# A two-layer trunk with product-key experts on one core: operands of the expert selection in PSUM, sixteen conditioning items in an earlier stage, and the last norm dealt to more engines

## The chip, the cores and the metric

The kernel runs on one core of a Trainium2 chip. The metric is the device time of one execution in microseconds. The engines are named as in the profile: PE (TensorE), DVE (VectorE), ACT (ScalarE), POOL (GpSimd), SP (SyncE, which here issues most of the DMAs).

## What is computed

The model takes 256 prompt tokens and 32 sample tokens of width 1024 through two layers, all in float32. Cut to what matters here:

```python
for l in range(2):
    mod = silu(c) @ ada_w[l] + ada_b[l]              # 1024 x 6144 per layer, for two vectors c
    sh1, sc1, g1, sh2, sc2, g2 = split(mod, 6)
    h = modulate(rmsnorm(x, norm_mix[l]), sh1, sc1)
    x = x + g1 * (rglru_block(h) if l == 0 else conformer_conv_block(h))
    h = modulate(rmsnorm(x, norm_ffn[l]), sh2, sc2)
    x = x + g2 * peer(h)
y = rmsnorm(x, norm_final)

def peer(h):                                         # 8 heads, 128 + 128 keys, 16384 experts
    q = h @ w_q
    s1v, s1i = top_k(q[first half] @ k1.T, 16);  s2v, s2i = top_k(q[second half] @ k2.T, 16)
    sv, si = top_k(s1v[:, None] + s2v[None, :], 16)  # 16 of 256 pairs
    e = s1i[si // 16] * 128 + s2i[si % 16]
    return sum over the 16 of  softmax(sv) * gelu(u[e] . h) * v[e]
```

The kernel does not gather experts for the prompt. It computes z = h U^T for all 16384 experts, multiplies by a gate that is zero except at the selected ones, and multiplies by V. Only the sample tokens are gathered.

## The kernel before

**Items.** The program is one list of items, each of which brings a block of weights (512 KB for most) and multiplies it. `run_stream` walks the list as a pipeline: `load` issues the DMA on SP into one of three `raw` buffers; `prep`, two items ahead, transposes on DVE (z items, L955); `split`, one item ahead, makes a rounded high part on ACT (`hi`, L332) and the rest on POOL or DVE (`lo`, L333); then PE multiplies (hi by hi and lo, lo by hi, L342; for v items L1089); then `post` follows. The order in which Python emits instructions is each engine's order. Dependencies become semaphore waits.

**Threads.** Small side work (a list of operations with an engine, a cost and the number of items to wait before the next, the "hop") is emitted between items by `run_threads`, within a budget of time per engine and item.

**Conditioning.** `ada_unit(l, u, ring)` makes eight items for one of the six 1024-column parts of `ada_w[l]`: each has a load of 512 KB (L399) and two small products (L406); after the eighth a thread of copies (ACT), transposes (PE) and additions (DVE) finishes the part. These items have rings of their own (`rb` nine slots, `rc` six) and no place in the list: `with_ada(items, units, {k: n}, {k: (n, ahead)})` hangs n of them behind item k ("riding"), or n in front of it ("lead"). A riding item's load is issued when a slot is free, that is, when PE has read the slot's former content.

**The stages.** First 16 ada items. Then layer 0's LRU stage `d`: 8 items for the recurrent half of `w_in`, 8 for its gate half, 8 for `w_out`; ada items ride on items 2 to 9, and 8 lead item 16, the first of `w_out`. Then `peer_items(0, ...)`: 128 z items, which multiply the rows of U; behind each of z items 1 to 8 come two items of `w_q`, after which a thread takes the top 16 of one head and half; from z item 9 on, two ada items ride on each while there are some left. Here these are 24 (parts 5 of layer 0, 0 and 1 of layer 1): seven lead z item 0, seventeen ride.

**Selection.** When all top-16 results are there, the thread of `select_ops` runs while z items go on: candidates (POOL), top 16 of them (DVE), `conv` (subtracts the maximum, L776), the exponential (ACT), `start1` (L783 to L792), steps that turn positions into keys (L798, L801), `soft` (L811), `ints` (L818 to L822), `start2` (from L826), the same steps for the second key, two transposes (PE), `parts` (which splits the gate into mantissa and exponent, L856 to L862, and copies a constant, `iota4`) and `fin`, which starts 64 groups of gate work (L913). Its arrays are 128 x 288 and lie in `scr`, in SBUF; two of them, `far["pos"]` and `far["tmp"]`, lie in PSUM. Every operation is made in two halves.

**Experts down and the end.** 128 v items follow; four PSUM accumulators `acc[tt][half]` hold 128 tokens by 512 columns. The last two v items hold back the products for tt = 1, and after those for tt = 0 do them half by half. In layer 1, after the last item, each of the four quarters gets its gate, residual (`sums`: L1198, L1201) and squares (L1204, ACT); `inv_rms` makes 1/rms (L1213, L1215); `weighted` multiplies by the norm's weight (L1853), `y_out` by 1/rms (L1856, L1858), and three stores go out on SP (L1878, L1882). Layer 1 is built in the same way; where its own ada items stand is not changed.

## Time and profile before

| | |
|---|---|
| three runs | 2065.05, 2055.79, 2060.77 us; median 2060.77 |
| profiled execution | 2065.36 us; its span 2063.6 us, granted clock 0.989 |
| PE busy | 1989.8 us, 96% of the span (13603 instructions) |
| PE weight loads | 1718.6 us, 83% |
| DVE | 1534.8 us, 74% (3324) |
| ACT | 1113.3 us, 54% (1973) |
| POOL | 993.7 us, 48% (644) |
| read from memory | 434.19 MB, 213 GB/s over the span |

The profiled execution is one on the chip, a little longer than the median of the three. A view of windows gives, for stretches of time, how long each engine was busy, the granted clock of PE and the DMA engines' mean busy share. A timeline lists instructions with their start, their duration, how many were joined into a row and, in brackets, how long the engine stood before and what released it. A view of lines groups the instructions of the whole run by their line in the program.

### The profile page before, as it was taken

Reading aid. Unit: us, or ns where it says so; the run is one execution under the profiler, and the core shown is the slowest. Engines: PE = TensorE matmul, PEld = TensorE weight load, DVE = VectorE, ACT = ScalarE, POOL = GpSimd, SP = SyncE. Lnnn points to the kernel's source line nnn. Section 1 sums busy time; section 2 is a strip of 40 time slices with the busy share of each in tenths; the row PEclk is TensorE's granted clock in tenths of the full one; section 3 lists DMA queues with packets and bytes.
Section 4 is the critical chain, followed back from the end, with each engine's and each line's share of the span. In section 5 each row is a group of like instructions: output and inputs, shape, how many; then the busy total and the mean of one; then the engine's idle time right before and its main releaser. Section 6 shows DMA issues by size and latency. Waiting matters only on the chain.

```text
span 2063.6 us, 38013 instructions
## 1 busy us (share of the span) xinstructions
PE 1989.8 (96%) x13603; PEld 1718.6 (83%) x13603; DVE 1534.8 (74%) x3324; ACT 1113.3 (54%) x1973; POOL 993.7 (48%) x644
## 2 busy tenths in 40 slices
PE   6989999999999999999999899999999999999998
PEld 4777978999999887777877679999999988777776
DVE  5785559999998876455658855799999978754455
ACT  3655434478886444344554544444888854444444
POOL 4346667777775232121245266877777743312100
PEclk9999999999999999999999999999999999999999
DMA  9856595555556988887686455665555578878863
GB/s 341 274 180 217 142 247 163 168 171 158 156 155 220 314 297 284 291 278 235 236 271 163 148 161 147 179 174 164 169 158 155 157 259 315 296 276 293 277 202 124
DMA packets 311483, 444.44 MB, mean 215 GB/s; under 512 B 29326, under 2 KB 248126, under 8 KB 310782
## 3 DMA queue, kind: packets, MB, share of 16 engines
q1 hardware_dynamic: 292142, 374.73, 57.6%
q0 software_dynamic: 18976, 67.22, 9.4%
q8 instruction: 107, 1.75, 0.4%
q14 instruction: 82, 0.67, 0.1%
q10 hardware_dynamic: 176, 0.07, 0.0%
HBM read 434.19 MB, written 4.87 MB: 213 GB/s over the span
## 4 chain that ended last, share of the span: by engine, by line
PE 65%; DVE 11%; issue 9%; DMA 8%; POOL 5%; ACT 2%; SPq 1%; DVEq 0%; ACTq 0%; POOLq 0%
PE b L342 34%; PE acc L1089 21%; DVE ut L955 3%; PE acc L913 3%; POOL scr L996 3%; POOL lo L333 2%; DMA raw<-in_peer_u_dram 2%; DMA raw<-in_peer_v_dram 2%; PE b L1033 1%; DMA big<-in_ada_w_dram 1%; DVE lo L333 1%; ACT hi L332 1%; PE acc L406 1%; DMA scr<-in_peer_u_dram,eidx 1%; DVE acc L798 1%
## 5 line engine op out<-in xcount | busy, mean ns | idle before, releaser
L342 PE MATMUL b<-rnd,hi 128*128 128x256 f32 (+1 forms) x5376 | 737.9, 290 | 19.7 <-ACT hi L332 10.8
L333 POOL TENSOR_TENSOR lo<-ut,hi 128x1024 fp32r<-128x1024 f32 x253 | 608.1, 2406 | 231.7 <-PE b L342 122.2
L342 PEld LDWEIGHTS b<-rnd,hi 128*128 128x128 f32 x5376 | 681.1, 190 | 42.2 <-ACT hi L332 15.8
L332 ACT CAST hi<-raw 128x1024 fp32r<-128x1024 f32 x336 | 353.1, 1052 | 396.7 <-DMA raw<-in_peer_v_dram 234.0
L1089 PE MATMUL acc<-hi,rnd 128*128 128x512 f32 x2048 | 557.6, 393 | 2.9 <-ACT hi L332 2.7
L333 DVE TENSOR_TENSOR lo<-raw,hi 128x1024 fp32r<-128x1024 f32 x282 | 348.1, 1236 | 265.0 <-PE acc L1089 124.7
L1089 PEld LDWEIGHTS acc<-hi,rnd 128*128 128x128 f32 x2048 | 380.2, 188 | 111.9 <-issue 23.4
L955 DVE STREAM_TRANSPOSE ut<-raw 128x1024 f32<-128x1024 f32 x256 | 317.0, 1239 | 129.4 <-DMA raw<-in_peer_u_dram 97.2
L342 PE MATMUL b<-rnd,lo 128*128 128x256 f32 (+1 forms) x2688 | 386.4, 285 | 9.6 <-POOL lo L333 5.2
L342 PEld LDWEIGHTS b<-rnd,lo 128*128 128x128 f32 x2688 | 351.2, 189 | 14.3 <-POOL lo L333 8.8
L332 ACT CAST hi<-ut 128x1024 fp32r<-128x1024 f32 x256 | 269.5, 1053 | 172.2 <-DVE ut L955 148.8
L1089 PE MATMUL acc<-lo,rnd 128*128 128x512 f32 x1024 | 317.7, 391 | 1.7 <-DVE lo L333 1.3
L1089 PEld LDWEIGHTS acc<-lo,rnd 128*128 128x128 f32 x1024 | 191.2, 188 | 46.6 <-DVE lo L333 6.8
L1023 POOL DMA_INDIRECT big<-in_peer_v_dram,eidx x64 | 65.6, 1025 | 266.0 <-PE b L1033 252.8
L333 POOL TENSOR_TENSOR lo<-raw,hi 128x1024 fp32r<-128x1024 f32 x54 | 129.9, 2407 | 113.0 <-PE b L342 60.1
L996 POOL DMA_INDIRECT scr<-in_peer_u_dram,eidx x64 | 84.2, 1316 | 187.3 <-DVE scr L1000 186.6
L907 ACT ACTIVATE scr<-scr 128x128 bf16<-128x128 bf16 x512 | 169.3, 407 | 0.0
L976 ACT ACTIVATE big<-b 128x512 f32<-128x512 f32 (+32 forms) x123 | 59.8, 486 | 73.4 <-PE b L342 73.2
L1000 DVE SCALAR_TENSOR_TENSOR scr<-scr 128x1024 f32<-128x1024 f32 x64 | 78.1, 1221 | 25.9 <-DMA scr<-in_peer_u_dram,eidx 25.7
L1064 DVE TENSOR_TENSOR rnd<-big,rnd 128x512 fp32r<-128x512 f32 x128 | 89.9, 702 | 4.1 <-ACT rnd L1063 4.1
L913 PE MATMUL acc<-scr 128*128 128x128 bf16 x1024 | 81.9, 223 | 0.0
L1063 ACT CAST rnd<-big 128x512 fp32r<-128x512 f32 x128 | 78.8, 615 | 4.0 <-PE b L342 4.0
(316 smaller groups left out, 1593.6 us busy)
## 6 DMA issues: line engine op xcount, KB each, us to landing
raw<-in_peer_u_dram SPq DMA_DIRECT2D x1024, 128.0 KB
raw<-in_peer_v_dram SPq DMA_DIRECT2D x256, 512.0 KB
big<-in_ada_w_dram SPq DMA_DIRECT2D x96, 512.0 KB
raw<-in_peer_w_q_dram SPq DMA_DIRECT2D x128, 128.0 KB
raw<-in_cf_w_pw_dram SPq DMA_DIRECT2D x24, 512.0 KB
raw<-in_lru_w_in_dram SPq DMA_DIRECT2D x16, 512.0 KB
raw<-in_lru_w_out_dram SPq DMA_DIRECT2D x8, 512.0 KB
xsave<-big SPq DMA_DIRECT2D x2, 1152.0 KB
```

The lines of the kernel that those rows point to most:

```text
L332: S.copy(hi, src)
L333: (G if pool_lo else V).tensor_tensor(lo, src, hi.bitcast(F32), op=ALU.subtract)
L342: TE.matmul(ps, w[wi][:, c * P:(c + 1) * P], a[ai][:, c, :n], start=(start and wi == c == ai == 0), stop=(stop and wi == 1 and c == C - 1))
L907: S.activation(bt[:, j], b4[:, :, j], AF.Copy, scale=sexp[:, t0 + j:t0 + j + 1])
L913: TE.matmul(s["ps"][:, j * P:(j + 1) * P], a[:, :, j], bt[:, j], start=a is hi, stop=a is lo)
L955: V.transpose(s["ut"].rearrange("p (b e n) -> p e b n", b=8, e=4), s["raw"].rearrange("p (e b n) -> p e b n", e=4, b=8))
L996: G.indirect_dma_start(out=gt, out_offset=None, in_=Uf, in_offset=bass.IndirectOffsetOnAxis(ap=eidx[:, s:s + 1], axis=0))
L1000: V.scalar_tensor_tensor(gt, gt, 1.0, hs_v, op0=ALU.mult, op1=ALU.mult, accum_out=zs[:, s:s + 1])
L1023: G.indirect_dma_start(out=gt[j], out_offset=None, in_=Vf, in_offset=bass.IndirectOffsetOnAxis(ap=eidx[:, s + j:s + j + 1], axis=0))
L1063: S.copy(w[0], src)
L1064: V.tensor_tensor(w[1], src, w[0].bitcast(F32), op=ALU.subtract)
L1089: TE.matmul(acc[tt][half], w[a][:, c0:c0 + P], s["w"][b][:, half * 512:(half + 1) * 512], start=(i == 0 and a == 0 and b == 0), stop=(i == ...
```

## The change

It has three parts.

1. In `select_ops`, for both layers: the casts of `k1` and `k2` to float (L783, L785) become two copies on ACT behind the exponential, and `start1` comes one item later. One operand of several DVE operations moves to PSUM: the maximum (`far["red"]`), the result of `start1`'s fused operation and the operands of its difference, the integer keys (`far["int"]`), the bits of the gate (`far["bits"]`). One copy (L822) goes, one is new (two halves, from PSUM to `k1`). `iota4` is copied by ACT.
2. Part 5 of layer 0 and part 0 of layer 1 of `ada_w`, 16 items, move to the LRU stage: ada items ride on items 2 to 15, and 12 lead item 16. One part, eight items, is left for the z items: seven lead, one rides.
3. The last two v items are done half by half for both token tiles. In the last norm POOL makes three of four weightings; the first tile's halves are scaled by DVE; in the second ACT scales one half, and one fused operation on DVE makes the weight and the scale of the other; its two stores go out from two queues, ACT's and SP's.

```diff
         def select_ops():
...
+                b0, b1 = bank(True), bank(True)
+                far["pos"], far["tmp"], far["int"] = in_psum(b0), in_psum(b1), in_psum(b1.bitcast(I32))
+                far["red"] = b0[:, NA:NA + NH]
+                far["bits"] = b0[:, :NP], b1[:, :NP]
                 for a in hh:
                     V.tensor_copy(far["pos"][:, a], ci[:, a])
-                    V.tensor_copy(smx[:, a], sv[:, a, 0])
+                    V.tensor_copy(far["red"][:, a], sv[:, a, 0])
                 for a in hh:
-                    V.tensor_tensor(sv[:, a], sv[:, a], smx[:, a].unsqueeze(2).to_broadcast(bc), op=ALU.subtract)
+                    V.tensor_tensor(sv[:, a], sv[:, a], red(a), op=ALU.subtract)
+
+            def exp():
+                S.activation(sv, sv, AF.Exp)
+                for n in range(2):
+                    S.copy(idxf[n], idxs[n])
             add("V", 1.1, conv)
-            add("S", 0.5, lambda: S.activation(sv, sv, AF.Exp), 1)
+            add("S", 1.3, exp, 1)
             def start1():
+                t = far["tmp"]
                 for a in hh:
-                    V.tensor_copy(k1[:, a], idxs[0][:, a])
-                for a in hh:
-                    V.tensor_copy(k2[:, a], idxs[1][:, a])
-                for a in hh:
-                    V.scalar_tensor_tensor(k1[:, a], k1[:, a], 64.0, offs.unsqueeze(1).to_broadcast(bc),
+                    V.scalar_tensor_tensor(t[:, a], k1[:, a], 64.0, offs.unsqueeze(1).to_broadcast(bc),
                                            op0=ALU.mult, op1=ALU.add)
                 for a in hh:
-                    V.tensor_tensor(dl[:, a, 1:], k1[:, a, 1:], k1[:, a, :15], op=ALU.subtract)
+                    V.tensor_copy(k1[:, a], t[:, a])
+                for a in hh:
+                    V.tensor_tensor(dl[:, a, 1:], t[:, a, 1:], k1[:, a, :15], op=ALU.subtract)
...
-            add("V", 2.1, start1, 0)
+            add("V", 1.6, start1, 1)
...
             def soft():
                 V.tensor_reduce(smx, sv, axis=AX.X, op=ALU.add)
-                V.reciprocal(smx, smx)
+                V.reciprocal(far["red"], smx)
                 for a in hh:
-                    V.tensor_tensor(sv[:, a], sv[:, a], smx[:, a].unsqueeze(2).to_broadcast(bc), op=ALU.mult)
+                    V.tensor_tensor(sv[:, a], sv[:, a], red(a), op=ALU.mult)
             def ints():
+                ia = far["int"]
...
-                for a in hh:
-                    V.tensor_copy(tmp[:, a], ib[:, a])
             def start2():
                 for a in hh:
-                    V.tensor_copy(i1[:, a], ia[:, a])
+                    V.tensor_copy(i1[:, a], far["int"][:, a])
                 for a in hh:
-                    V.tensor_tensor(far["pos"][:, a], far["pos"][:, a], tmp[:, a], op=ALU.subtract)
+                    V.tensor_tensor(far["pos"][:, a], far["pos"][:, a], ib[:, a], op=ALU.subtract)
...
             def ev(tt):
...
+                    if tt == 1:
+                        S.copy(iota4, iota.unsqueeze(2).to_broadcast([P, P, 4]))
             def parts():
-                V.tensor_copy(iota4, iota.unsqueeze(2).to_broadcast([P, P, 4]))
+                man, ex = far["bits"]
...
-                V.tensor_scalar(gate.bitcast(I32), gate.bitcast(I32), 0x7F800000, None, op0=ALU.bitwise_and)
+                V.tensor_scalar(ex.bitcast(I32), gate.bitcast(I32), 0x7F800000, None, op0=ALU.bitwise_and)
...
+                if i < ET - 2:
+                    for tt in range(2):
                         mms(tt, (0, 1))
-                    elif tt == 0:
-                        mms(tt, (0, 1))
-                        late.append(mms)
-                if i == ET - 1:
-                    for half in range(2):
-                        for f in late:
-                            f(1, (half,))
+                    return
+
+                late.append(mms)
+                if i == ET - 2:
+                    mms(0, (0,))
+                    return
+                for k, (tt, half) in enumerate(((0, 0), (0, 1), (1, 0), (1, 1))):
+                    for f in late[0 if k else 1:]:
+                        f(tt, (half,))
...
-    with_ada(d, a01, {k: 2 for k in range(2, 10)}, {16: (8, 0)})
+
+    a01 += ada_unit(0, 5, rb) + ada_unit(1, 0, rb)
+    with_ada(d, a01, {k: 2 for k in range(2, 16)}, {16: (12, 0)})
     items += d
-    a1 = ada_unit(0, 5, rc) + [it for u in range(2) for it in ada_unit(1, u, rc)]
+    a1 = ada_unit(1, 1, rc)
...
-    for m, a, q in ((m00, a00, q00), (m01, a01, q01), (m10, a10, q10), (m11, a11, None)):
+    for m, a, q in ((m00, a00, q00), (m01, a01, q01), (m10, a10, q10)):
         m()
         a(V)
-        if q is not None:
-            q()
+        q()
+    weighted(0, 0, G)
     weighted(0, 1, G)
-    weighted(0, 0, G)
+    weighted(1, 0, G)
     n01()
+    m11()
+    a11(V)
     q11()
-    weighted(1, 0, V)
     n02()
-    weighted(1, 1, V)
+    V.tensor_scalar(ZT[:, 0, HALF[0]], ZT[:, 0, HALF[0]], r0, None, op0=ALU.mult)
     n11()
-    y_out(0, 0, r0)
-    y_out(0, 1, r0)
+    V.tensor_scalar(ZT[:, 0, HALF[1]], ZT[:, 0, HALF[1]], r0, None, op0=ALU.mult)
     nc.sync.dma_start(y_p[0, :P], ZT[:, 0])
     n12()
-    for h in range(2):
-        y_out(1, h, r1)
-        nc.sync.dma_start(y_p[0, P:, HALF[h]], ZT[:, 1, HALF[h]])
+
+    S.activation(ZT[:, 1, HALF[0]], ZT[:, 1, HALF[0]], AF.Copy, scale=r1)
+    V.scalar_tensor_tensor(ZT[:, 1, HALF[1]], XTC[:, 1, HALF[1]], r1, NFR[:, HALF[1]], op0=ALU.mult, op1=ALU.mult)
+    nc.scalar.dma_start(y_p[0, P:, HALF[0]], ZT[:, 1, HALF[0]])
+    nc.sync.dma_start(y_p[0, P:, HALF[1]], ZT[:, 1, HALF[1]])
```

The change moves instructions at three places. On SP, in the LRU stage, before (`big` holds the rings of the ada items, `raw` the stream's buffers):

```order
L399 DMA big<-in_ada_w_dram 128x1024 x2
L367 DMA raw<-in_lru_w_in_dram 128x8x128
L399 DMA big<-in_ada_w_dram 128x1024
L367 DMA raw<-in_lru_w_in_dram 128x8x128 x2
L367 DMA raw<-in_lru_w_out_dram 128x8x128 x5
L624 DMA scr<-in_peer_k_dram 128x128 x2
```

and with the change:

```order
L399 DMA big<-in_ada_w_dram 128x1024 x2
L367 DMA raw<-in_lru_w_in_dram 128x8x128
L399 DMA big<-in_ada_w_dram 128x1024 x2
L367 DMA raw<-in_lru_w_out_dram 128x8x128
L399 DMA big<-in_ada_w_dram 128x1024 x2
L367 DMA raw<-in_lru_w_out_dram 128x8x128
```

In this way it goes on: from there, five raw loads of `w_out` in all stand each behind a pair of ada loads, where they stood one behind another, and three more ada loads follow the fifth, ahead of the keys.

On DVE, in layer 0's selection, from `conv` to the end of `start1`, before (`ut` is a z item's transposed block, `smx` the maximum):

```order
L774 COPY smx<-scr 128x9
L776 TENSOR_TENSOR scr<-scr,smx 128x144 x2
L955 STREAM_TRANSPOSE ut<-raw 128x4x8x32 x2
L783 CAST scr<-scr 128x144 x2
L785 CAST scr<-scr 128x144 x2
L787 SCALAR_TENSOR_TENSOR scr<-scr,offs 128x144 x2
L790 TENSOR_TENSOR scr<-scr 128x9x15 x2
L792 COPY scr<-scr 128x144 x2
```

and with the change (`acc` is PSUM):

```order
L778 COPY acc<-scr 128x9
L780 TENSOR_TENSOR scr<-scr,acc 128x144 x2
L964 STREAM_TRANSPOSE ut<-raw 128x4x8x32 x2
L793 SCALAR_TENSOR_TENSOR acc<-scr,offs 128x144 x2
L796 COPY scr<-acc 128x144 x2
L798 TENSOR_TENSOR scr<-acc,scr 128x9x15 x2
L800 COPY scr<-scr 128x144 x2
```

The two casts are gone from between the transposes, and the subtraction and the difference have one operand in PSUM.

On DVE, at the program's end, before:

```order
L1198 TENSOR_TENSOR acc<-acc,big 128x512
L1201 TENSOR_TENSOR big<-big,acc 128x512
L1213 TENSOR_TENSOR tst<-tst 128x1
L1853 TENSOR_TENSOR big<-big 128x512
L1215 RECIPROCAL tst<-tst 128x1
L1853 TENSOR_TENSOR big<-big 128x512
L1213 TENSOR_TENSOR tst<-tst 128x1
L1858 TENSOR_SCALAR big<-big,tst 128x512
L1215 RECIPROCAL tst<-tst 128x1
L1858 TENSOR_SCALAR big<-big,tst 128x512 x2
```

and with the change:

```order
L1224 TENSOR_TENSOR tst<-tst 128x1
L1209 TENSOR_TENSOR acc<-acc,big 128x512
L1212 TENSOR_TENSOR big<-big,acc 128x512
L1226 RECIPROCAL tst<-tst 128x1
L1882 TENSOR_SCALAR big<-big,tst 128x512
L1224 TENSOR_TENSOR tst<-tst 128x1
L1884 TENSOR_SCALAR big<-big,tst 128x512
L1226 RECIPROCAL tst<-tst 128x1
L1889 SCALAR_TENSOR_TENSOR big<-big,tst 128x512
```

Behind the last quarter's addition stand two multiplications by 1/rms and one fused operation, where two weightings and three multiplications stood.

## Rows read from the trace of the kernel before

**Rows 1.** Windows: stretches from and to, length, busy time per engine.

```profile
core 0: us, PE busy (x) PEld busy (x) DVE busy (x) ACT busy (x) POOL busy (x), PEclk, DMA share, GB/s
45.00:80.00 35.00, 35.00 (x239) 27.67 (x239) 31.51 (x70) 21.03 (x44) 14.56 (x32) 1.00 1.04 361
90.20:123.20 33.00, 25.03 (x183) 20.95 (x181) 31.64 (x49) 24.83 (x53) 22.18 (x19) 0.99 0.43 126
263.60:303.10 39.50, 38.82 (x299) 28.90 (x299) 20.58 (x85) 14.69 (x26) 24.52 (x18) 1.00 1.00 260
317.70:432.40 114.70, 106.48 (x873) 103.56 (x872) 106.60 (x259) 52.74 (x69) 86.12 (x37) 1.00 0.58 165
1402.50:1406.20 3.70, 3.61 (x17) 3.61 (x18) 3.44 (x10) 1.58 (x3) 3.59 (x2) 0.54 0.86 247
```

**Rows 2.** Timeline of PE at both selections: start, duration, instruction, count.

```profile
317.71 2.03 PE L342 MATMUL b<-rnd,hi 128*128 128x256 f32 x16
...
432.39 0.64 PE L913 MATMUL acc<-scr 128*128 128x128 bf16 x8
...
1311.63 2.03 PE L342 MATMUL b<-rnd,hi 128*128 128x256 f32 x16
...
1351.02 2.03 PE L342 MATMUL b<-rnd,hi 128*128 128x256 f32 x16
...
1450.08 2.14 PE L342 MATMUL b<-rnd,hi 128*128 128x256 f32 x16
```

**Rows 3.** Lines of DVE, whole run: shapes, count, busy us, mean ns, idle before.

```profile
L801 DVE TENSOR_TENSOR scr<-scr,acc 128x144 f32<-128x144 f32 x120 | 31.1, 300 | 2.0
...
L776 DVE TENSOR_TENSOR scr<-scr,smx 128x144 f32<-128x144 f32 x4 | 5.4, 1396 | 0.0
...
L859 DVE TENSOR_SCALAR scr<-scr 128x256 int32<-128x256 int32 x2 | 4.9, 2428 | 0.1
...
L826 DVE CAST scr<-scr 128x144 f32<-128x144 int32 x4 | 4.1, 1066 | 0.0
...
L811 DVE TENSOR_TENSOR scr<-scr,smx 128x144 f32<-128x144 f32 x4 | 4.0, 1037 | 0.1
...
L790 DVE TENSOR_TENSOR scr<-scr 128x135 f32<-128x135 f32 x4 | 3.2, 834 | 0.0
...
L785 DVE CAST scr<-scr 128x144 f32<-128x144 uint32 x4 | 2.9, 772 | 0.0
```

**Rows 4.** Timeline of DVE: the second key's casts in layer 0 and layer 1.

```profile
333.03 2.56 DVE L785 CAST scr<-scr 128x144 f32<-128x144 uint32 x2
...
1353.46 0.37 DVE L785 CAST scr<-scr 128x144 f32<-128x144 uint32 x2
```

**Rows 5.** Timeline of POOL at the first of these.

```profile
332.94 2.42 POOL L333 TENSOR_TENSOR lo<-ut,hi 128x1024 fp32r<-128x1024 f32 x1 [2.53 <-ACT hi L332]
```

**Rows 6.** Timeline of PE: z items with riders, and the LRU stage's lead and `w_out`.

```profile
115.32 3.64 PE L406 MATMUL acc<-big,scT 128*32 128x512 f32 x32
...
123.20 3.59 PE L342 MATMUL b<-rnd,hi 128*128 128x288 f32 x15 [3.92 <-DVE rnd L496]
...
265.57 2.14 PE L342 MATMUL b<-rnd,hi 128*128 128x256 f32 x16
...
303.13 2.03 PE L342 MATMUL b<-rnd,hi 128*128 128x256 f32 x16
```

**Rows 7.** Timeline of DVE at the program's end.

```profile
2050.62 0.70 DVE L1198 TENSOR_TENSOR acc<-acc,big 128x512 f32<-128x512 f32 x1 [1.70 <-PE acc L1089]
...
2058.07 0.88 DVE L1858 TENSOR_SCALAR big<-big,tst 128x512 f32<-128x512 f32 x2
```

**Rows 8.** Timeline of SP's queue: the last two stores.

```profile
2058.91 1.15 SPq L1882 DMA_DIRECT2D out_dram<-big  x2
```

**Rows 9.** Chain of work that ended last: start, duration; v items' products in layer 1.

```profile
1835.77 8.39 PE acc L1089 x36
```

**Rows 10.** Timeline of ACT at the end of layer 0's v items.

```profile
1040.15 1.05 ACT L332 CAST hi<-raw 128x1024 fp32r<-128x1024 f32 x1 [3.93 <-PE acc L1089]
```

More of the change, by code (lines that the diff above doesn't have):

```diff
@@ L740, in select_ops @@
             cand = scr[:, o:o + NH * NCAND].rearrange("p (h k) -> p h k", h=NH)
-            ia, ib = hk(o, NA, I32), hk(o + NA, NA, I32)
-            tmp = hk(o + 2 * NA, NA)
+            ib = hk(o + NA, NA, I32)
             o += NH * NCAND
@@ L751, in select_ops, with in_psum @@
             far = {}
-            def in_psum():
-                return bank(True)[:, :NA].rearrange("p (h k) -> p h k", k=TOPK)
+            def in_psum(b):
+                return b[:, :NA].rearrange("p (h k) -> p h k", k=TOPK)
             bc = [P, NH // 2, TOPK]
             ops = []
+            red = lambda a: far["red"][:, a].unsqueeze(2).to_broadcast(bc)
             def add(eng, cost, fn, *hop):
@@ L836, in select_ops @@
                 add("V", 1.75, steps(i2, [(k, k) for k in range(r, min(r + 2, TOPK))]), 0)
-            gate, man = scr[:, 4 * NP:5 * NP], scr[:, 5 * NP:6 * NP]
+            gate = scr[:, 4 * NP:5 * NP]
             def tr(tt):
@@ L852, in f @@
                     S.copy(gate[:, tt * P:(tt + 1) * P], pt[:, 2 * P:3 * P])
+                    if tt == 1:
+                        S.copy(iota4, iota.unsqueeze(2).to_broadcast([P, P, 4]))
                 return f
             def parts():
-                V.tensor_copy(iota4, iota.unsqueeze(2).to_broadcast([P, P, 4]))
+                man, ex = far["bits"]
                 V.tensor_scalar(man.bitcast(I32), gate.bitcast(I32), 0x007FFFFF, 0x44800000,
                                 op0=ALU.bitwise_and, op1=ALU.bitwise_or)
-                V.tensor_scalar(gate.bitcast(I32), gate.bitcast(I32), 0x7F800000, None, op0=ALU.bitwise_and)
+                V.tensor_scalar(ex.bitcast(I32), gate.bitcast(I32), 0x7F800000, None, op0=ALU.bitwise_and)
                 V.tensor_copy(smant[:, 0], man)
-                V.tensor_scalar(sexp, gate, 1.0 / 1024, None, op0=ALU.mult)
+                V.tensor_scalar(sexp, ex, 1.0 / 1024, None, op0=ALU.mult)
                 V.tensor_tensor(smant[:, 1], man, smant[:, 0], op=ALU.subtract)
@@ L1071, in pe @@
                 st["nv"] = i
-                for tt in range(2):
-                    if i < ET - 2:
+                if i < ET - 2:
+                    for tt in range(2):
                         mms(tt, (0, 1))
-                    elif tt == 0:
-                        mms(tt, (0, 1))
-                        late.append(mms)
-                if i == ET - 1:
-                    for half in range(2):
-                        for f in late:
-                            f(1, (half,))
+                    return
[6 more added lines that the diff above has]
+                        f(tt, (half,))
             def mms(tt, halves):
@@ L1853, in weighted @@
         eng.tensor_tensor(ZT[:, tt, HALF[h]], XTC[:, tt, HALF[h]], NFR[:, HALF[h]], op=ALU.mult)
-    def y_out(tt, h, rs):
-        z = ZT[:, tt, HALF[h]]
-        if tt or h:
-            V.tensor_scalar(z, z, rs, None, op0=ALU.mult)
-        else:
-            S.activation(z, z, AF.Copy, scale=rs)
     n01, n02, r0 = inv_rms(0, 1)
     n11, n12, r1 = inv_rms(1, 2)
-    for m, a, q in ((m00, a00, q00), (m01, a01, q01), (m10, a10, q10), (m11, a11, None)):
+    for m, a, q in ((m00, a00, q00), (m01, a01, q01), (m10, a10, q10)):
         m()
         a(V)
-        if q is not None:
-            q()
+        q()
+    weighted(0, 0, G)
     weighted(0, 1, G)
-    weighted(0, 0, G)
+    weighted(1, 0, G)
     n01()
+    m11()
+    a11(V)
     q11()
-    weighted(1, 0, V)
     n02()
-    weighted(1, 1, V)
+    V.tensor_scalar(ZT[:, 0, HALF[0]], ZT[:, 0, HALF[0]], r0, None, op0=ALU.mult)
     n11()
-    y_out(0, 0, r0)
-    y_out(0, 1, r0)
+    V.tensor_scalar(ZT[:, 0, HALF[1]], ZT[:, 0, HALF[1]], r0, None, op0=ALU.mult)
     nc.sync.dma_start(y_p[0, :P], ZT[:, 0])
     n12()
-    for h in range(2):
-        y_out(1, h, r1)
-        nc.sync.dma_start(y_p[0, P:, HALF[h]], ZT[:, 1, HALF[h]])
+    S.activation(ZT[:, 1, HALF[0]], ZT[:, 1, HALF[0]], AF.Copy, scale=r1)
+    V.scalar_tensor_tensor(ZT[:, 1, HALF[1]], XTC[:, 1, HALF[1]], r1, NFR[:, HALF[1]], op0=ALU.mult, op1=ALU.mult)
+    nc.scalar.dma_start(y_p[0, P:, HALF[0]], ZT[:, 1, HALF[0]])
+    nc.sync.dma_start(y_p[0, P:, HALF[1]], ZT[:, 1, HALF[1]])
 _INS = ['x_prompt', 'x_sample', 'c_prompt', 'c_sample', 'state_lru_h', 'state_lru_conv', 'state_dwconv', 'ada_w', 'ada_b',
```

1 line of the change is left out of this document (removed).

## Prediction

> **What bounds the kernel now.** I read the page's busy times first: TensorE (PE) is busy for 1989.8 of 2063.6 us and its clock is full nearly throughout. What a change saves must therefore be time in which PE stands, or runs slower than it could. So I went to the windows view, stage by stage, and looked for stretches where something else sets PE's pace. There are three, and the change touches each.
>
> *Selection* (top-16 and what follows it). Without it a z item takes PE 2.814 us: 14 items between the starts 1311.63 and 1351.02 [rows 2]. In layer 0's selection 36 items lie between 317.71 and 432.39, 114.68 us; 36 x 2.814 = 101.3, its own transposes take about 0.6, so 12.8 us are lost. In layer 1, 31 items lie between 1351.02 and 1450.08, 99.06 us; 87.2 and about 1.0 of other products leave 10.8 lost. Together 23.6. The engine at its limit there is DVE: 106.60 of 114.70 us busy, with ACT at 52.74 and POOL at 86.12 [rows 1].
>
> *The z items on which ada items ride.* From 265.57 to 303.13 [rows 6], 37.56 us, PE does 9 z items (25.3 us), and 12.2 us pass beyond them. Seventeen ada items ride there, and an ada item's products take 3.64/8 = 0.455 us [rows 6]: 7.7 us of the 12.2 are these products, the rest is slower going. The DMA engines are at share 1.00 there [rows 1], so that stretch is also at the limit of its transfers.
>
> *The LRU stage's end.* Between 90.20 and 123.20, PE is busy for 25.03 of 33.00 us and DMA at 0.43, 126 GB/s [rows 1]: both have room. It ends in a 3.92 us wait for DVE [rows 6].
>
> **Part A, the selection.** The edits take operands of DVE's instructions out of SBUF. What such an instruction costs with one operand in PSUM is shown by the steps' own addition L801: 300 ns for 128x144 [rows 3]. The same kind of work wholly in SBUF costs 1396 (L776), 1037 (L811), 1066 (L826), 772 (L785) and, for 128x256, 2428 ns (L859) [rows 3]. Why is seen at L785: in layer 0 two of them take 2.56 us, beginning at 333.03 and ending at 335.59, just after POOL's lo operation, 332.94 + 2.42 = 335.36 [rows 4, 5]; in layer 1 the same two take 0.37 us [rows 4]. The DVE instruction stands while POOL works. Those five groups are 5.4 + 4.0 + 4.1 + 2.9 + 4.9 = 21.3 us [rows 3]. L776, L811, L826 and L859 stay, 14 instructions at 0.3 = 4.2; L785 goes to ACT; the new copy is 4 x 0.3 = 1.2. That frees 21.3 - 5.4 = 15.9 us of DVE, and L818 and L822 a little more. Not all of it reaches PE, since the sixty steps, which are not touched, still come in lumps among DVE's transposes. I take **-14**. Bounds: 0, if the lumps alone set the loss, and -23.6, if all loss goes. At one place more than the instruction comes back: at 1402.50 PE ran 3.61 us for 17 products at a granted clock of 0.54 [rows 1], where 16 take 2.03 us elsewhere [rows 2]: 1.5 us after a wait that the freed DVE should not cause.
>
> ACT takes two casts per layer and the copy of iota4. None can be dearer than the 128x1024 cast, 1.05 us [rows 10]: at most 3.2 us per layer, against 62 us in which ACT is idle [rows 1]. Behind them in ACT's queue stand the hi casts that PE needs; one displaced by 1.05 us is covered by the item that is ahead of PE. The start of the steps now waits for ACT, but is emitted an item later, so that DVE's transposes stand between and nothing queues behind that wait: 0.
>
> **Part B, the moved ada items.** Sixteen (8.39 MB) leave the z stage for the LRU stage. One still rides. The z stage gets back its 12.2 us and about 0.5 of waits at the items after it, less 0.5 for that one: **-12.2**. The LRU stage gets 16 x 0.455 = 7.3 us of products, and has 33.00 - 25.03 = 8.0 us of idle PE, 3.92 of it in one piece at the place where four of them are added to the lead (1.8 us). It also gets the bytes: 126 GB/s x 33 us = 4.16 MB, with 8.39 makes 12.55. What this DMA can carry, the stretch from 45 to 80 us shows: 361 GB/s [rows 1]. 12.55 MB take 34.8 us at that, 1.8 more than the stage has. With some 0.7 for the small copies, transposes and additions at the end of two more units I take **+2.5**. Bounds: -1.2, if keeping PE at work gives back the clock (the products at 123.20, right after the wait, take 3.59 us for 15 [rows 6]), and +23.2, if all 8.39 MB stand exposed at 361 GB/s. Net **-9.7**. On SP the raw loads of this stage now stand behind ada pairs; the last three lead loads wait for the first three lead products, since the ring has nine slots: three loads are 1.57 MB, 4.4 us, covered by the six products between (2.7 us) and the 3.92 us wait, from which the last products come off too.
>
> **Part C, the last two v items and the end.** A v product takes 8.39/36 = 0.233 us [rows 9]. Half by half, DVE's first addition, at 2050.62 [rows 7], can begin five products earlier, 1.17 us. But the last half ends with PE, so DVE's chain gains about 1.1. Behind it, one fused operation stands where the two multiplications took 0.88 us [rows 7]; the other half is ACT's beside it, some 0.3. The two last stores took 1.15 us to issue from one queue [rows 8]; from two, the second leaves some 0.5 earlier. **-2.0**, bounds 0 and -2.5 (all three at their whole size would be more, but they overlap). The half order applies to layer 0's last v items too: 0 there, for ACT's hi cast, which waits for PE 3.93 us and begins at 1040.15 [rows 10], stands ahead of the squares in ACT's queue.
>
> **Sum.** -14 - 9.7 - 2 = **-25.7**. The profiled execution took 2065.36, which gives 2039.7; the median of the runs, 2060.77, is 4.6 less and gives 2035.1. I say **2037**; its own band is 2030 to 2044.
>
> **Rivals.**
> 1. *The blocking stays, on the instructions that still have two inputs in SBUF.* Start1's fused operation, start2's difference of k2 and the last address operation are not moved out. For it: L790, with both inputs in SBUF, averages 834 ns where L801 takes 300 [rows 3]. Against: part of these are in layer 1, where L785 ran undisturbed [rows 4]. Price: up to 2.56 - 0.37 = 2.2 us [rows 4] at two places in two layers, 8.8, so part A falls to about 5: **2046**. It decides if those instructions start while a lo operation of POOL is under way. The Trainium skill (SBUF — State Buffer, "Who interferes with whom") says that a DVE instruction with two SBUF inputs contends with a GpSimd instruction that reads SBUF, and that the later one blocks wholly. By that rule the fused operation and the difference would go on standing; L785, which has one input, stood as well in our trace, so the rule's list of such instructions has to be read together with its next point, that casts can take the shared ports too.
> 2. *The LRU stage's transfers take back what was moved.* It decides if the 12.55 MB run below 361 GB/s, for at 270 GB/s, near the 260 of the z stage [rows 1], they take 46.5 us, 13.5 more than the stage has, where the sum has 2.5; the 11 between are all of part B: **2048**. For: the z stage with the same mixture of loads shows that 260 at a share of 1.00. Against: from 45 to 80 us ada and raw loads together ran at 361.
> 3. *Both*: **2057**, no difference that can be told.
> 4. *Slower: SP's queue becomes a convoy.* Eight raw loads (three of w_in, five of w_out) each stand behind an ada pair whose slot is free only when PE has used it, and PE waits for the raw load behind. If each then costs PE its pair and itself, 1.57 MB or 4.4 us, 8 x 4.4 = 35, with 4.4 for the last three lead loads 39.6, less the 28.2 gained elsewhere: 11 us slower, **2072**. It decides if a raw load lands more than about 12 us after the load before it: that is its lead over PE, three buffers at some 4 us an item (33.00 us for eight). Against: nine slots are nearly five pairs of slack.
> 5. *Better*: all of selection's 23.6 returns: **2027**.
>
> That the change does not do what it says is possible in one place, layer 0's half order, and is in the sum as 0.
>
> **How the numbers follow.** Forecast 0.58, rival 1 0.14, rival 2 0.12, both 0.04, convoy 0.04, better 0.08. The range holds the forecast's band, rivals 1 and 2 and most of "better": **2026 to 2050**; outside lie both, the convoy, the far side of rivals 1 and 2 and a little of "better", near 0.2. A measurement of this kernel can tell about 0.5% from no change, here 10.3 us. Below 2050.5 lie the forecast, "better" and most of rivals 1 and 2: faster 0.82; the rest of those and "both" 0.14; the convoy 0.04.
>
> **What the profile after would show.** Right: the moved groups near 300 ns, 36 items from the start of layer 0's selection within about 107 us, and no full stop of PE after its first top-16 results; z items after W_q at 2.82 us with DMA well below 1.00; the LRU stage with DMA near 1.00, PE at w_out within 3 us of 123.20; the last store issued about 2 us earlier after PE's last product. Wrong: idle time before the ada products L406, or before ACT's cast of w_in and w_out, named DMA (rivals 2 and 4); two-input SBUF instructions of 1 to 2.5 us in the steps' starts (rival 1). If DVE's time in selection falls and PE's pitch there does not, the lumps set it and part A was my mistake.

## The result and the profile after

The changed kernel takes 2053.03 us (median of 17 runs, 2049.01 to 2056.43), the kernel before 2065.76 (17 runs, 2055.79 to 2071.12). The ratio is 0.9943, 95% interval 0.9931 to 0.9954: 12 us faster, where 24 to 26 were forecast, and outside the range of 2026 to 2050. A ratio, here and below, is taken over all runs of both kernels; it is not exactly the quotient of the two medians. The page of the changed kernel begins:

```profile
span 2052.8 us, 37998 instructions
## 1 busy us (share of the span) xinstructions
PE 1989.0 (97%) x13603; PEld 1716.1 (84%) x13603; DVE 1520.4 (74%) x3312; ACT 1113.3 (54%) x1979; POOL 999.4 (49%) x646
```

DVE lost 14.4 us of busy time, PE's work is the same, and the span is 10.8 us shorter. Where this comes from is read from PE's timelines: both kernels run the same items in the same order, so the start of one item in one trace, less its start in the other, shows what has been won or lost up to there. The table has the differences to the kernel before; the change's column is the one to look at first, the others are the experiments below.

| up to the item that in the kernel before starts at | change | only_a | only_b | b_turns | b_lead8 | b_one | a_psum2 | two_psum2_fixed |
|---|---|---|---|---|---|---|---|---|
| 90.17 (LRU stage, `w_in`) | +0.7 | +0.6 | +0.8 | +1.4 | +0.5 | +0.4 | -0.3 | +0.6 |
| 127.68 (second item of `w_out`) | +9.5 | +0.7 | +9.8 | +10.9 | +3.7 | 0.0 | +8.1 | +2.0 |
| 149.97 (last of `w_out`) | +16.2 | +0.6 | +16.4 | +11.0 | +7.4 | -0.1 | +14.7 | +4.3 |
| 265.57 (first z item with riders) | +16.8 | +0.5 | +16.9 | +12.0 | +7.8 | -0.3 | +14.4 | +1.0 |
| 309.00 (after the riders) | +4.9 | +1.1 | +5.1 | +0.1 | -4.1 | -7.0 | +2.5 | -10.9 |
| 436.21 (layer 0's first gates) | -0.9 | -4.1 | +2.9 | -6.0 | -10.1 | -12.9 | -7.6 | -21.3 |
| 659.56 (first v item) | -1.5 | -5.9 | +2.2 | -6.6 | -10.8 | -14.1 | -8.2 | -21.9 |
| 1052.23 (layer 1's first item) | -4.7 | -6.1 | -2.9 | -10.5 | -11.4 | -17.0 | -14.1 | -24.4 |
| 1339.77 (z items before selection) | -5.7 | -6.4 | -4.2 | -11.4 | -12.1 | -17.7 | -15.1 | -26.0 |
| 1446.10 (layer 1's first gates) | -9.3 | -9.9 | -4.1 | -15.0 | -15.7 | -21.3 | -22.7 | -33.6 |
| 2044.71 (last v items) | -8.8 | -8.9 | -5.4 | -15.9 | -16.4 | -23.1 | -24.8 | -35.2 |
| span's end (2063.6) | -10.8 | -8.9 | -5.4 | -17.9 | -18.4 | -25.1 | -26.8 | -37.2 |

The gains of the change are there: the z items with riders win 11.9 us (from +16.8 to +4.9), the two selections some 6 and 4, the end 2.0. Layer 0's v items are 3.2 us shorter, which nobody forecast. Against them stands one loss, 16 us in the LRU stage, most of it after 110 us. What that stage looks like now, in the windows view of the changed kernel (the second window is the stretch of the kernel before from 90.20 to 123.20 [rows 1]; the last is layer 0's selection):

```profile
core 0: us, PE busy (x) PEld busy (x) DVE busy (x) ACT busy (x) POOL busy (x), PEclk, DMA share, GB/s
45.00:80.00 35.00, 35.00 (x239) 27.68 (x238) 31.40 (x70) 21.19 (x45) 14.44 (x32) 1.00 1.02 352
90.85:133.94 43.09, 38.41 (x250) 22.87 (x249) 34.66 (x63) 26.65 (x59) 22.23 (x19) 0.96 0.90 306
123.00:126.00 3.00, 1.23 (x6) 0.29 (x8) 2.93 (x13) 1.71 (x4) 0.40 (x1) 1.00 1.06 408
126.00:130.00 4.00, 2.05 (x10) 0.26 (x8) 0.97 (x6) 0.00 (x0) 0.00 (x0) 1.00 1.08 400
130.00:135.00 5.00, 5.00 (x20) 1.46 (x19) 0.00 (x0) 0.00 (x0) 0.00 (x0) 0.66 0.34 124
135.00:140.00 5.00, 5.00 (x40) 5.00 (x39) 2.35 (x4) 0.00 (x0) 0.00 (x0) 1.00 0.00 0
...
322.30:431.50 109.20, 105.54 (x872) 103.20 (x872) 101.31 (x281) 51.38 (x65) 85.31 (x37) 1.00 0.59 172
```

The DMA engines carry 306 GB/s on the mean, below the 352 of the stretch from 45 to 80 us. From 123 to 130 us they are full (share 1.06 and 1.08), while PE is busy for 3.28 of 7 us; from 135 to 140 they carry nothing at all, and ACT is idle from 130 to 140. So bytes alone don't bound the stage: in one place PE waits for them, and in another something keeps the loads and the casts from being issued. PE's timeline of the changed kernel shows the first half of the loss, in the lead of twelve ada items:

```profile
118.93 3.64 PE L406 MATMUL acc<-big,scT 128*32 128x512 f32 x24
123.11 1.05 PE L406 MATMUL acc<-big,scT 128*32 128x512 f32 x4 [0.55 <-DMA big<-in_ada_w_dram]
125.83 1.05 PE L406 MATMUL acc<-big,scT 128*32 128x512 f32 x4 [1.66 <-DMA big<-in_ada_w_dram]
127.09 1.05 PE L406 MATMUL acc<-big,scT 128*32 128x512 f32 x4 [0.21 <-DMA big<-in_ada_w_dram]
129.88 4.13 PE L406 MATMUL acc<-big,scT 128*32 128x512 f32 x12 [1.74 <-DMA big<-in_ada_w_dram]
133.94 2.37 PE L342 MATMUL b<-rnd,hi 128*128 128x288 f32 x16
```

`w_out` begins at 133.94 instead of 123.20 [rows 6]. DVE had the rounded activations ready at 126.6; after that PE waits only for the last lead items' loads. The waits for loads in the lead add up to 4.2 us. Behind them the granted clock is 0.66 on the mean from 130 to 135 us, so in part at the lower of its two levels, 1.2 GHz, and the last twelve products take 4.13 us, where the first 24 took 3.64. The last three loads go out at 122.88, behind a pair (118.44) and a raw load that has to wait for its buffer (122.41):

```profile
118.44 1.31 SPq L399 DMA_DIRECT2D big<-in_ada_w_dram  x2
122.41 0.38 SPq L367 DMA_DIRECT2D raw<-in_lru_w_out_dram  x1
122.88 1.90 SPq L399 DMA_DIRECT2D big<-in_ada_w_dram  x3
```

The second half is on ACT (timelines of the changed kernel, ACT's and then PE's):

```profile
124.72 0.42 ACT L418 COPY arow<-acc 128x128 f32<-128x128 f32 x2
144.05 0.43 ACT L418 COPY arow<-acc 128x128 f32<-128x128 f32 x2 [18.90 <-PE acc L412]
...
145.75 1.04 ACT L332 CAST hi<-raw 128x1024 fp32r<-128x1024 f32 x1
...
155.88 0.43 ACT L418 COPY arow<-acc 128x128 f32<-128x128 f32 x2 [6.42 <-PE acc L412]
...
157.73 1.04 ACT L332 CAST hi<-raw 128x1024 fp32r<-128x1024 f32 x1
```

```profile
146.84 3.85 PE L342 MATMUL b<-rnd,hi 128*128 128x288 f32 x16 [1.22 <-ACT hi L332]
```

With twelve leading, two ada units end together, and two finishing threads start at once. Each begins with two copies on ACT into `arow`, which has two buffers. The first thread's copies fill both; the second's stand behind them in ACT's queue until PE has transposed the first two (L412), and PE's order has these after three items of `w_out`. Behind the blocked copies stand ACT's squares and the cast of `w_out`'s fourth item, for which PE waits in the last row (and then takes 3.85 us for 16 products, where the first of `w_out` took 2.37); behind that cast stands DVE's lo operation, and behind that SP's next raw load. In the kernel before only one unit ended there.

In selection the moved groups fell as forecast, and three others rose (lines of DVE in the changed kernel, whole run; L780 was L776, L798 was L790 and L833 was L826 [rows 3], L837 was L830, L793 was L787, L880 was L871):

```profile
L837 DVE TENSOR_TENSOR scr<-scr 128x135 f32<-128x135 f32 x4 | 7.2, 1826 | 0.0
L793 DVE SCALAR_TENSOR_TENSOR acc<-scr,offs 128x144 f32<-128x144 f32 x4 | 5.3, 1321 | 0.1
...
L880 DVE SCALAR_TENSOR_TENSOR scr<-scr 128x32 f32<-128x32 f32 x2 | 3.3, 1652 | 0.0
...
L780 DVE TENSOR_TENSOR scr<-scr,acc 128x144 f32<-128x144 f32 x4 | 1.0, 300 | 0.1
...
L798 DVE TENSOR_TENSOR scr<-acc,scr 128x135 f32<-128x135 f32 x4 | 1.0, 288 | 0.0
...
L833 DVE CAST scr<-acc 128x144 f32<-128x144 int32 x4 | 1.0, 280 | 0.0
```

Before, L787 took 294 ns, L830 290 and L871 182. These are the fused operation of `start1`, the difference of `start2` and the last address operation in `fin`, the three that still have both inputs in SBUF and that rival 1 named: 10.2 us of waiting came back on DVE at the first two, and 2.9 at the third. It is POOL again, as in [rows 4, 5]; in the changed kernel's DVE and POOL timelines the pair of L837 in layer 0 ends, at 384.62 + 3.75 = 388.37, just after POOL's two lo operations, at 383.39 + 4.82 = 388.21:

```profile
384.62 3.75 DVE L837 TENSOR_TENSOR scr<-scr 128x135 f32<-128x135 f32 x2
```

```profile
383.39 4.82 POOL L333 TENSOR_TENSOR lo<-ut,hi 128x1024 fp32r<-128x1024 f32 x2 [0.94 <-ACT hi L332]
```

At the end, 8.0 us lie between PE's last product and the span's end, instead of 10.1; the last stores leave from two queues, and the fused operation takes 0.75 us where two multiplications took 0.88 [rows 7, 8] (timelines of DVE, ACT's queue and SP's queue):

```profile
2047.82 0.75 DVE L1889 SCALAR_TENSOR_TENSOR big<-big,tst 128x512 f32<-128x512 f32 x1
```

```profile
2048.63 0.38 ACTq L1890 DMA_DIRECT2D out_dram<-big  x1
```

```profile
2048.59 0.34 SPq L1891 DMA_DIRECT2D out_dram<-big  x1
```

### The profile page after: what moved, and what is told of

Same layout as the page of the kernel before. It is cut to its first block, busy times and chain, and to the rows that moved or that the text cites. A ratio compares the mean times of both kernels' runs of the same rounds, so it can differ in the third digit from the quotient of the medians.

```text
span 2052.8 us, 37998 instructions
## 1 busy us (share of the span) xinstructions
PE 1989.0 (97%) x13603; PEld 1716.1 (84%) x13603; DVE 1520.4 (74%) x3312; ACT 1113.3 (54%) x1979; POOL 999.4 (49%) x646
## 4 chain that ended last, share of the span: by engine, by line
PE 69%; DVE 10%; issue 8%; POOL 7%; DMA 4%; ACT 2%; SPq 0%; DVEq 0%; ACTq 0%; POOLq 0%
PE b L342 34%; PE acc L1100 24%; DVE ut L964 4%; POOL lo L333 4%; PE acc L922 3%; POOL scr L1005 3%; PE acc L406 2%; PE b L1042 2%; DMA raw<-in_peer_u_dram 1%; ACT hi L332 1%; DMA scr<-in_peer_u_dram,eidx 1%; DMA big<-in_ada_w_dram 1%; DVE lo L333 1%; PE b L712 1%; PE b L1723 1%
## 5 line engine op out<-in xcount | busy, mean ns | idle before, releaser
L342 PE MATMUL b<-rnd,hi 128*128 128x256 f32 (+1 forms) x5376 | 735.4, 289 | 12.1 <-ACT hi L332 5.8
L342 PEld LDWEIGHTS b<-rnd,lo 128*128 128x128 f32 x2688 | 350.6, 188 | 10.5 <-POOL lo L333 9.4
L985 ACT ACTIVATE big<-b 128x512 f32<-128x512 f32 (+16 forms) x124 | 60.2, 486 | 66.4 <-PE b L342 66.1
```

The source lines that it names most:

```text
L342: TE.matmul(ps, w[wi][:, c * P:(c + 1) * P], a[ai][:, c, :n], start=(start and wi == c == ai == 0), stop=(stop and wi == 1 and c == C - 1))
```

## Experiments: the parts alone

Here are four kernels with the hunks of one part, or of two, on the kernel before. Here and below, each was run in five rounds against the kernel before.

**only_a**, the hunks in `select_ops` alone.

> Part A alone (selection) on the kernel before. Theory 1, from the two traces: selection gains 5.8 us in layer 0 and 3.8 in layer 1, nothing elsewhere: about 9.6 less than before, ratio 0.9953. Theory 2, the selection's gain needs the LRU stage's other order: under 5, ratio above 0.9975. If the 3.9 us that layer 0's gates and v items lost are A's too, 13.5, ratio 0.9935.

Measured: 2056.9 us, ratio 0.9957 (0.9934 to 0.998). The interval reaches past the second theory's 0.9975, so the profile decides, in which layer 0's selection gains 5.1 us and layer 1's 3.5 with the LRU stage as before. Selection alone gains nearly what was expected, and the theory that it needs the LRU stage's order falls.

**only_b**, the hunk at `with_ada` alone.

> Part B alone (sixteen ada items moved) on the kernel before. Theory 1: the LRU stage grows by 16.1 us and the z items with riders shrink by 11.9, so about 4 us slower than before, ratio 1.002. Theory 2, the slow LRU stage was an accident of one profiled execution: the sum of the prediction, 9.7 faster, ratio 0.9953.

Measured: 2062.18, ratio 0.9984 (0.9964 to 1.0004). Neither theory's ratio came (1.002 and 0.9953). By the stages the first theory holds to a few tenths, +16.1 and -11.9 us, so the loss in the LRU stage is no accident. The time is no slower than before, since layer 0's selection (1.9) and its v items (5.1) are shorter in that profile; the v items differ between profiles that have the same instructions there (-0.2 in only_a), so that this is not put down to part B.

**only_c**, the hunks in `v_item` and after `run_stream`.

> Part C alone (last two v items, last norm) on the kernel before. Both theories: 2 us faster at the end, ratio 0.999, not told from no change by the time; the profile should show the distance from the last v product's start to the span's end shorter by about 2 us, and layer 0's end unchanged.

Measured: 2062.7, ratio 0.9978 (0.9956 to 1.0), which by itself can't be told from no change. In its profile the time from PE's last product to the span's end is 8.0 us, as in the change, and layer 0's end has not moved.

**a_and_c**, the change without part B.

> The change without part B. Theory 1: B costs 4 us net, so this is about 4 us faster than the whole change, 15 to 17 less than before, ratio 0.992 to 0.993. Theory 2 (B gains 9.7): 2 to 3 us less than before, ratio 0.9987.

Measured: 2054.83, ratio 0.9946 (0.9926 to 0.9966), against 0.9943 for the whole change. Neither number came: in the time, part B is worth nothing that can be told as it stands, neither 4 us lost nor 10 gained.

## Experiments: the LRU stage

**b_turns** lets the finishing threads take turns.

```diff
-                                       ("V", 0.4, fin)]))
+                                       ("V", 0.4, fin)], group=("ada", 1)))
```

> The whole change, with the threads that finish an ada unit taking turns (one at a time), so that ACT is never given a second unit's copies while both row buffers are full. Loads and products of PE unchanged. Theory 1 (ACT's queue): the 18.90 us and 6.42 us waits of ACT's copies for PE's transposes go, w_out's casts come on time, the LRU stage is 5 to 7 us shorter, ratio to before about 0.991. Theory 2 (transfers): those casts wait for raw loads all the same, stage unchanged, ratio 0.994. In both, the start of w_out stays some 9 us later than before.

Measured: 2043.43, ratio 0.9895 (0.9869 to 0.9921). ACT's copies no longer wait, and the cast of the fourth item comes at 141.43 instead of 145.75 (its timeline):

```profile
125.48 0.42 ACT L418 COPY arow<-acc 128x128 f32<-128x128 f32 x2
...
141.43 1.05 ACT L332 CAST hi<-raw 128x1024 fp32r<-128x1024 f32 x1
...
144.62 1.05 ACT L332 CAST hi<-raw 128x1024 fp32r<-128x1024 f32 x1
```

Up to the last item of `w_out` 5.1 us are won, and the start of `w_out` stays late, at +10.9. The second theory falls. Of the 10 us of the time, 5 are in this stage; the rest lies in stretches that this edit doesn't touch, and within the intervals.

**b_lead8** keeps the lead at eight and the order of loads on SP.

```diff
-    with_ada(d, a01, {k: 2 for k in range(2, 16)}, {16: (12, 0)})
+    with_ada(d, a01, {k: 2 for k in (*range(2, 16), 17, 18)}, {16: (8, 0)})
```

> The whole change, with 8 leading ada items as before and the other four riding on w_out's second and third item. SP's order of loads stays the same. Theory 1: PE's 7 us of waits inside the lead for the last loads go, and the two units no longer end together, so ACT's long wait goes too: LRU stage 9 to 13 us shorter than in the change, ratio to before 0.988 to 0.990. Theory 2 (the stage is bound by 12.55 MB of transfers): PE waits for the same bytes at w_out's raw loads instead, at most 3 us gained, ratio 0.993.

Measured: 2045.51, ratio 0.9903 (0.9876 to 0.993). The stage is 8.8 us shorter than in the change, just short of the 9 to 13 of the first theory; the second, with at most 3, falls. The lead now ends at 126.6 (PE's timeline):

```profile
122.78 1.05 PE L406 MATMUL acc<-big,scT 128*32 128x512 f32 x4 [0.19 <-DMA big<-in_ada_w_dram]
125.59 1.05 PE L406 MATMUL acc<-big,scT 128*32 128x512 f32 x4 [1.75 <-DMA big<-in_ada_w_dram]
126.57 3.91 PE L342 MATMUL b<-rnd,hi 128*128 128x288 f32 x16
```

The same bytes are loaded in the same order, and PE does other work while the last ones come. What was lost came from the place of four products in PE's order: the transfers can run beside other work.

**b_one** moves part 5 of layer 0 only, with a lead of eight and nine riders left for the z items.

> The whole change with only one unit moved (part 5 of layer 0, eight items); part 0 of layer 1 goes back to the z items. Lead of 8 as before. Theory 1: the LRU stage costs 2 to 4 us instead of 16, the z items get back 6 to 7 of the 12: about 6 faster than the change, ratio 0.991. Theory 2 (cost in proportion to bytes): half of each, 8 and 6, so 2 faster, ratio 0.9935.

Measured: 2044.87, ratio 0.9907 (0.988 to 0.9933). The LRU stage costs nothing at all (-0.3 at the first z item with riders), and 6.7 us of the z items' 12 come back. Cost in proportion to bytes falls: the first unit is free, and the second costs all 16 us as the change places it.

## Experiments: the blocking in selection

**a_psum2** gives two of the three risen operations, L793 and L837, one input in PSUM.

```diff
+                far["offs"] = b0[:, NA + NH:NA + NH + TOPK]
+                V.tensor_copy(far["offs"], offs)
...
-                    V.scalar_tensor_tensor(t[:, a], k1[:, a], 64.0, offs.unsqueeze(1).to_broadcast(bc),
+                    V.scalar_tensor_tensor(t[:, a], k1[:, a], 64.0, far["offs"].unsqueeze(1).to_broadcast(bc),
...
+                t = far["tmp"]
+                for a in hh:
+                    V.tensor_copy(t[:, a], k2[:, a])
                 for a in hh:
-                    V.tensor_tensor(dl[:, a, 1:], k2[:, a, 1:], k2[:, a, :15], op=ALU.subtract)
+                    V.tensor_tensor(dl[:, a, 1:], t[:, a, 1:], k2[:, a, :15], op=ALU.subtract)
```

> The whole change, with the two operations that still had both inputs in SBUF given one in PSUM: the table offs is copied there for start1's fused operation (L793), and k2 is copied there for start2's difference (L837). Theory 1 (blocking by POOL): they fall from 1321 and 1826 ns to about 300, DVE loses about 9 us of busy time, and selection is 3 to 6 us shorter in both layers together, ratio to before about 0.992. Theory 2 (the steps' lumps set the pace): durations fall, time does not, ratio 0.994. Theory 3: the next operation in SBUF takes the blocking over, so durations fall here and rise at L800 and L839.

Measured: 2040.19, ratio 0.9886 (0.9858 to 0.9913). Both fall to a quarter or less (its lines of DVE; L885 is the address operation in `fin`, with two inputs in SBUF still, and stands at 1670 ns, as in the change with 1652; L844 was L839):

```profile
L885 DVE SCALAR_TENSOR_TENSOR scr<-scr 128x32 f32<-128x32 f32 x2 | 3.3, 1670 | 0.0
...
L795 DVE SCALAR_TENSOR_TENSOR acc<-scr,acc 128x144 f32<-128x144 f32 x4 | 1.2, 298 | 0.1
...
L842 DVE TENSOR_TENSOR scr<-acc,scr 128x135 f32<-128x135 f32 x4 | 1.0, 292 | 0.1
...
L844 DVE COPY scr<-scr 128x144 f32<-128x144 f32 x4 | 1.0, 291 | 0.0
```

Layer 0's 36 items take 104.8 us from start to start, where the change takes 109.2 and the kernel before 115.1; layer 1's 31 take 91.3, 95.3 and 99.1. So the blocking of these two cost 8.3 us of the two selections, and the second theory falls. Of the 23.6 us that selection lost in the kernel before, 6.0 are still there; what part of them the steps' lumps have, and what part L885, was not tested. The third theory falls: the copies within SBUF after them stay at 290 ns.

## Experiments: together

**one_psum2** is b_one with a_psum2's edit.

> Both mends together: one unit moved instead of two, and the two operations' second operand in PSUM. Theory 1, the causes are independent and add: against the whole change the LRU and z stages are 12 us shorter and the two selections 8 us, so about 20 us less than the change, ratio to before 0.984 to 0.987. Theory 2, they share a bound (what is won in one stage is given back in the next): ratio no better than 0.9886.

Measured: 2038.27, ratio 0.9884 (0.9862 to 0.9906), short of what the first theory expected. The selections win their 8 us again: 16.8 in both layers (from -5.2 to -14.4 and from -15.3 to -22.9 in PE's timeline), where b_one has 9.2. But against b_one the LRU stage is 2.1 us longer, layer 0's selection begins 2 us later for it, and the v items of layer 0 are 4.4 us longer, for which no cause was found; the ratio alone doesn't separate the theories.

**one_psum2_single** and **none_psum2_single** let one ada item ride on a z item instead of two, with nine and with seventeen riders.

```diff
-                z.extra = ada_list[:2]
-                del ada_list[:2]
+                z.extra = ada_list[:1]
+                del ada_list[:1]
```

> As one_psum2, with one ada item riding on a z item instead of two. Theory 1, pairs make the z items transfer-bound: nine riders cost 5.5 us now and 4.1 of products then, so 1 to 2 us shorter between the last W_q item and the selection. Theory 2, products alone set it: no difference. By time the two can't be told apart, by the stage they can.

> No ada item moved, seventeen riding singly on z items; the rest as one_psum2. Theory 1 (the price of a pair on a z item was the transfers): 17 x 0.455 = 7.7 us instead of 12.2, so about 2 us slower than one_psum2_single and the LRU stage as before. Theory 2: riders that reach into selection stop ACT or DVE there, 5 us or more slower.

Measured: 2042.5, ratio 0.9908 (0.9888 to 0.9929), and 2054.01, ratio 0.9962 (0.9944 to 0.998). Both theories on the nine fall: nine single riders give back 2.2 us of the z stage, where the same nine in pairs gave back 6.7. With seventeen, the first theory falls, and the "5 us or more" of the second came (11.5 beyond the nine), but for another reason in the main. PE's timelines tell it. A single item's products take as long as a pair's (none_psum2_single at 268.99, the change at 94.25):

```profile
268.99 1.05 PE L406 MATMUL acc<-big,scT 128*32 128x512 f32 x4
```

```profile
94.25 1.07 PE L406 MATMUL acc<-big,scT 128*32 128x512 f32 x8
```

An item's two products use two groups of 32 output rows, and the next item's the other two, side by side. Seventeen single riders are 17.9 us; up to the item that starts at 320.52 in the kernel before they cost 5.8 more than the 12.2 of the pairs, and layer 0's selection, into which the riders reach, then wins 3 us less than in a_psum2; whether these stopped ACT or DVE there was not looked into.

**two_psum2_fixed** is b_lead8 with b_turns' and a_psum2's edits: two units moved, nothing of the change undone.

> Two units moved as in the change, with 8 leading, four riding on w_out, and finishing threads in turns, and the second operands in PSUM. Theory 1: LRU stage 5 to 8 us longer than before (7.3 of products and the last loads), z items 11.9 shorter: 2 us slower than one_psum2 at most, ratio 0.986 to 0.989. Theory 2: without its stalls the moved work is hidden in the 8 us of idle PE, LRU stage at most 2 longer, this is the fastest of the four.

Measured: 2029.13, ratio 0.9843 (0.982 to 0.9865), the fastest of all, against 0.9943 for the change. Its LRU stage costs 4.3 us up to the last item of `w_out`, which is beyond the 2 of the second theory, and no more than 1.0 at the z items with riders: in the kernel before, PE waits for ACT's squares at the stage's end (its timeline), and here it doesn't. The second theory holds, nearly.

```profile
159.69 0.75 PE L545 MATMUL acc<-big,ones 128*128 128x288 f32 x2 [2.54 <-ACT big L560]
```

## Why the prediction was wrong, by its own steps

*The view of what bounds the kernel* was right: PE lost time in three stretches. Two of them gave time back; the third, the LRU stage, was to take the moved work nearly free and did not.

*Part B, LRU stage, +2.5: this step failed*, by 13.6 us, most of the miss: in the profile the span fell by 10.8 us instead of 25.7, 14.9 short; part A lacked 4.2 beside these 13.6, and about 3 came back in stretches that the sum didn't have, most of them in layer 0's v items. Its bounds (-1.2 to +23.2) held the measured +16.1, its reasons did not. I priced bytes and PE's products, and the runs show that order decided whether they cost anything: with all sixteen items still moved, and the order of loads on SP kept, two_psum2_fixed has +1.0. First, there are four more products in the lead. I had the last three loads leave as soon as three slots were free and hidden by six products and DVE's wait; they left only at 122.88, behind a raw load that waited for a buffer, and while they came, at a DMA share above 1.00, `w_out` stood behind them in PE's queue. From the lead's first product to `w_out`'s, 15.0 us pass instead of 7.9: 7.1 more; of the stage's loss up to the second item of `w_out`, 5.8 are gone in b_lead8. That they would have landed in time without the raw load before them was not tested. Second, the finishing threads: I counted their "small copies" at 0.7 us and did not ask what stands behind the second one in ACT's queue when two units end at once (5.1 us, gone in b_turns). The rest is small: 2.9 us were lost before the lead, where six more ada pairs at 1.07 stand in PE's order.

*Part B, z items, -12.2*: measured -11.9. The reading beside it was partly wrong. I took 7.7 us for products and the rest for transfers, by the lead's 0.455 us an item; between z items a pair takes 1.06 and an item on its own 1.05, and the six pairs and three single items of this stretch make 9.5, so most of the 12 was PE's own work, and a DMA share of 1.00 did not mean that PE waited for it.

*Part A, -14*: measured 6.0 and 3.8, 9.8 in all. The mechanism was right, and the size was taken down by rival 1, which I gave a chance of 0.14 beside the forecast rather than inside it: its price was 8.8 us, and a_psum2 shows 8.3. Without it part A gives 18, above my -14, so I had taken off too much for the steps' lumps. I weighed these instructions by their quiet rows: in the kernel before, L787 ran at 294 ns because POOL was idle just then. In layer 0 it ran in the pause between POOL's operation that ended at 335.36 [rows 5] and the next (timelines of DVE and of POOL in the kernel before):

```profile
335.51 0.51 DVE L787 SCALAR_TENSOR_TENSOR scr<-scr,offs 128x144 f32<-128x144 f32 x2
```

```profile
335.78 2.50 POOL L333 TENSOR_TENSOR lo<-ut,hi 128x1024 fp32r<-128x1024 f32 x1 [0.42 <-ACT hi L332]
```

L785 ahead of it had waited POOL's operation out, and L790 behind it met the next. In layer 1 POOL was idle from 1351.96 to 1354.49, and L787 ran at 1353.75. With L785 gone, L793 met an operation of POOL itself. The Trainium skill (SBUF — State Buffer, "Who interferes with whom") says that a DVE instruction with two inputs in SBUF and a GpSimd instruction that reads SBUF exclude each other, and that the later one stands for the whole of the first. The runs agree: 1321 and 1826 ns with two inputs in SBUF, 298 and 292 with one in PSUM, POOL's operations taking 2.4 us in both. The rule had named the instructions.

*Part C, -2.0*: measured -2.0 in sum; its three pieces were not measured apart. Layer 0's half order gave 0, as said.

*The time.* Of the 16.0 us between 2037 and 2053.03, 3 are the starting point: I placed the kernel before between 2060.77 and 2065.36, and its 17 runs have 2065.76.

*Rivals 2, 3 and 4.* Both signs that I had named for a wrong prediction came: idle time before L406 that names DMA, and two-input instructions of 1.3 to 1.8 us in the steps' starts. The time lies between rival 2's 2048 and the 2057 of "both", which had a chance of 0.04. By size it was both: 8.3 us for the 8.8 of rival 1, and 13.6 beyond the sum for the 11 of rival 2. Rival 2's mechanism is there in part, since the stage's transfers ran at 306 GB/s on the mean and PE waited in the lead while DMA was full, but not its reason, that the bytes must cost PE time: DMA was idle from 135 to 140 us, and two_psum2_fixed moves the same bytes for +1.0. Rival 4's convoy is not there: SP hardly waited for a slot of the ada ring that PE had to free, but for buffers of the stream (SP's waits in the changed kernel from 90 to 150 us: us in all, times, longest):

```profile
SPq L367 <- DVE lo L333: 22.8, 4, 14.0
...
SPq L399 <- PE acc L412: 2.2, 2, 1.6
SPq L399 <- PE acc L406: 0.7, 1, 0.7
```

*What stays open.* Layer 0's v items are up to 6 us shorter or 2 longer than before in profiles whose instructions there are much the same, 3.2 shorter in the change; this is not explained, and part of each comparison's interval.

## What to carry to other kernels

Work that moves into idle time brings its tail along: look at what its finishing steps put into each in-order queue, which buffers they share when two of them end at once, and what stands behind. When an instruction that waited is removed, the wait can go to the next one of its kind, as it did here, so price the whole run of such instructions and not each by its own row. A half-full engine and a half-full DMA say that there is room, and not that the order lets it be used: two of the three edits that mended this were a matter of one line each, and together with the third they are worth 1%.

## What the runs showed of the hardware that was not expected

Two ada items' products, 8 records, take 1.07 us together, one item's 4 records 1.05: products into different groups of 32 output rows run side by side, so riding singly doubles the price of an item. The Trainium skill has this in TensorEngine Tiling (Array Packing), "Key Properties": different tiles can work in parallel; the rows here agree. And one input in PSUM brought a DVE instruction of 128x135 from 1826 to 292 ns, while copies that stayed within SBUF kept 290 right behind it.
